# Tree levels in blocks of 64 keys by 32 queries, masked straight into place; the order around ring slots, the gate in the output weights and the last norm

## The chip, the cores and the metric

The kernel runs on one core of a Trainium2 chip. The metric is device time in microseconds (us) of one execution. Three runs of the kernel before took 2049.74 to 2051.89 us, median 2050.69 us.

## What is computed

One layer over 2048 tokens of width 1024, in float32. `proj = h @ w_in` makes queries, forget values and values for two paths of 8 heads each: a gated linear recurrence (HGRN2) and a retention with a fixed decay. Both are normed by head, gated, merged and sent through `w_out`; a last norm follows.

```
h    = rms_norm(x, norm_g) * (1 + scale) + shift      # shift, scale, gate from c
proj = h @ w_in
# HGRN2, by head:  S_t = diag(f_t) S_{t-1} + (1 - f_t) v_t^T ;  o_t = S_t^T q_t
#   inside a chunk:  A[t, s] = sum_d q[t,d] * decay[t,s,d] * k[s,d]   for s <= t
# retention, by head: the same with a fixed decay
m    = sigmoid(ga) * uA + sigmoid(gb) * uB
x    = x + gate * (m @ w_out)
out  = rms_norm(x, final_g)
```

## The kernel before

**Dense products.** All projections are 128x128 by 128x512 products on TensorE. A float32 number is split into a high and a low part (`hi` by ScalarE, `lo` by VectorE), and each product is three matmuls (`mm3`, lines 505 to 508). `x` is held in two super-blocks (`sb`) of 1024 tokens. For each of them and each of 4 pairs of heads (`p`), `do_pair` runs group `a` (forget values `gf` and queries `gq`), for even `p` group `b` (retention queries and keys of two pairs, `gr`), group `c` (values, `gv`) and two groups `d` (gates, `gg`). A group by tokens has 8 chunks of 128 tokens; one chunk is 24 matmuls into one of three PSUM banks (tag `pd`), and the last two chunks, 6 and 7, run side by side (`group_two`).

**The ring.** Weights come from HBM into two raw buffers and are split into a ring of 9 slots (`Ring.pump`). As chunk 7 uses up a slot, `release` calls `pump`, which splits a tile of the next group. In group `b` VectorE also reads the result out of PSUM by two products with cosines and sines (`rotate_products`, line 778); only then can the bank be used again. `tc.issue_after(i)` says that what is traced inside stands behind instruction `i` on that engine; what is not said so, a scheduler sorts.

**The tree.** Inside a chunk of 128 tokens the decay matrix of the recurrence is built in 7 levels, m = 1, 2, 4 ... 64 (`tree`, lines 584 to 697). At level m, the queries of each odd block of m tokens meet the keys of the even block before it; then VectorE multiplies `q` and `k` with the products of forget values in `f`, and the next level follows. The level's products go to the PSUM tile `lv` (one buffer). In code before, levels 1 to 8 multiply 32 keys with the 16 odd queries among the same 32 tokens: 64 matmuls for the 16 chunks of a pair, at 4 places of the array's columns (output rows 0, 32, 64, 96). Level 16 has 64 products of 16 keys by 16 queries at the same 4 places, level 32 has 32 products of 32 by 32 at 2 places, level 64 has 16 of 64 by 64 at 2 places. A mask `msk` keeps what belongs to a level: `copy_predicated` on VectorE writes it into `ad` (128 x 16 x 32), and at level 8 four copies on ScalarE put `ad` on the diagonal of `af` (128 x 16 x 128), the matrix that the recurrence's products read. Levels 16 to 64 go to `af` by copies on ScalarE.

**Between the dense matmuls.** `bg.tick` counts them, and at every ninth step a burst of small work is traced: a level of the tree, a step of the retention, a step of the recurrence. TensorE runs in this order, one behind the other.

**The end.** `out_half(t, nh)` multiplies the merged rows with one half of `w_out` (`ops`); VectorE multiplies the result with `gate`, adds it to `x`, ScalarE sums the squares, and at `nh == 1` follow the sum, a power -0.5 on GpSimd (`rstd_of`), two scalings on VectorE and two transfers. `load_wo(0)` is traced in the last group of gates and `load_wo(1)` behind the first two halves; the order of the halves is written out at line 1239.

Of the kernel before, what the change touches and what calls it, by code (L numbers as in the profile page):

```python
# [42 lines left out]
def tile_hybrid(ctx: ExitStack, tc: tile.TileContext, a: dict, out: bass.AP):  # L43
# [47 lines left out]
    def late_consts():  # L91
        m32 = upool.tile([P, 512], I32, name="m32", tag="sg", bufs=3)
        nc.sync.dma_start(out=m32[:, 0:66], in_=a["msk"])
        G.tensor_copy(
            out=msk, in_=m32[:, 0:64].rearrange("p (l t) -> p l t", l=4).unsqueeze(2).broadcast_to([P, 4, 16, 16])
        )
        G.tensor_copy(out=dmsk, in_=m32[:, 64:66].unsqueeze(1).broadcast_to([P, 16, 2]))
        for t, src in lates:
            nc.sync.dma_start(out=t, in_=src)
# [122 lines left out]
    msk = cpool.tile([P, 4, 16, 16], U8, name="msk", tag="msk")  # L222
    dmsk = cpool.tile([P, 16, 2], U8, name="dmsk", tag="dmsk")
# [6 lines left out]
    ad = cpool.tile([P, 16, 32], F32, name="ad", tag="ad")  # L230
    G.memset(ad, 0.0)
# [229 lines left out]
    class Ring:  # L461
        def __init__(self):
# [7 lines left out]
            self.lasts = []  # L470

# [27 lines left out]
        def release(self):  # L499
            self.nfree += 1  # L500
            self.pump()
# [82 lines left out]
    def tree(p, sb, f, k, q):  # L584
# [14 lines left out]
        for li in range(7):  # L599
# [11 lines left out]
            if m < 16:  # L611
                for c in range(NC):
                    for u in range(4):
                        t0 = c * P + u * 32
                        PE.matmul(
                            out=ps[32 * u : 32 * u + 32, c * 16 : (c + 1) * 16].rearrange("p (n m) -> p n m", m=m),
                            lhsT=k[:, t0 : t0 + 32],
                            rhs=q[:, t0 : t0 + 32].rearrange("p (n two m) -> p n two m", two=2, m=m)[:, :, 1, :],
# [3 lines left out]
            else:  # L622
                nr = 64 // m
                for n in range(NC * nr):
                    c, r0 = (n // nr, n % nr * 2 * m) if m < 64 else (n // 2, n % 2 * 64)
                    PE.matmul(
                        out=ps[r0 : r0 + m, c * m : (c + 1) * m], lhsT=km[:, n, 0, :], rhs=qm[:, n, 1, :],
# [14 lines left out]
            if m == 1:  # L642
                V.copy_predicated(
                    out=ad.rearrange("p c (w j) -> p c w j", w=2)[:, :, :, 0], mask=dmsk,
                    data=psd.rearrange("p (c w) -> p c w", w=2),
                )
            if m < 16:
                V.copy_predicated(
                    out=ad.rearrange("p c (n two m) -> p (c n) two m", two=2, m=m)[:, :, 1, :],
                    mask=msk[:, li].rearrange("p c (n m) -> p (c n) m", m=m),  # L650
                    data=ps[:, 0 : 16 * NC].rearrange("p (n m) -> p n m", m=m),
                )
# [6 lines left out]
            else:  # L659
                for r0 in range(0, P, 2 * m):  # L660
                    S.activation(
                        out=af[r0 : r0 + m, :, r0 + m : r0 + 2 * m],
                        in_=ps[r0 : r0 + m, 0 : NC * m].rearrange("p (c t) -> p c t", t=m), func=AF.Copy,
                    )
# [107 lines left out]
    def rotate_products(p, gc, ps):  # L772
# [4 lines left out]
        for dst, tab in ((qk, rot["cos"]), (tr, rot["sin"])):  # L777
            V.tensor_tensor(  # L778
# [4 lines left out]
            )  # L783
        return qk, tr
# [130 lines left out]
    def do_pair(sb, p, hook):  # L915
# [296 lines left out]
    def out_half(t, nh):  # L1212
# [13 lines left out]
        V.tensor_tensor(out=yt, in0=ps, in1=gate[nh], op=ALU.mult)  # L1226
        V.tensor_tensor(out=xt[nh], in0=xt[nh], in1=yt, op=ALU.add)
        S.activation(out=yt, in_=xt[nh], func=AF.Square, accum_out=ss[:, nh : nh + 1])
        if nh == 0:
            return  # L1230
# [117 lines left out]
```

## Time and profile before

| | |
|---|---|
| median of the runs shown | 2050.69 us |
| the profiled execution's own time | 2049.87 us |
| its span, first to last instruction | 2047.9 us |
| mean granted clock of TensorE | 0.998 |
| VectorE busy | 1076.9 us (53%) |
| matmuls of `q` and `k` on `lv` in one tree (a float32 product is two instructions in the trace) | 736 |

The profile is of one execution. Its span is 2.0 us below the time of that execution, which is in turn 0.8 us below the median. In its rows PE is TensorE's matmuls, PEld its weight loads, DVE is VectorE, ACT ScalarE, POOL GpSimd, SP the engine that issues the transfers. In a timeline, a row gives the start, the duration, engine, line, operation, output and inputs, and how many instructions it merges; the bracket holds the idle time ahead of it and what ended that.

### The profile page before, as it was taken

How to read it: one execution, taken by the hardware profiler on the slowest of the kernel's cores; microseconds unless marked ns; L12 is line 12 of the kernel's file. 1: busy time of each engine (PE TensorE's matmuls, PEld its weight loads, DVE VectorE, ACT ScalarE, POOL GpSimd, SP SyncE). 2: the span in 40 equal slices, each digit the busy share in tenths (PEclk: the TensorE clock that was granted, in tenths of full speed). 3: DMA queues.
4: the chain of work that ended last, by engine and by line, in shares of the span. 5: the costliest groups of instructions: out<-in, count | busy, mean ns of one | idle time of the engine just before them, and what ended most of it. 6: DMA issues, size and time to landing. Idle time of an engine off the chain costs nothing.

```text
span 2047.9 us, 38316 instructions
## 1 busy us (share of the span) xinstructions
PE 2029.0 (99%) x15480; PEld 1674.4 (82%) x15480; DVE 1076.9 (53%) x2409; ACT 590.6 (29%) x1429; POOL 145.2 (7%) x262
## 2 busy tenths in 40 slices
PE   8999999999999999999999999999999999999998
PEld 6887888888888888888888888888878888888886
DVE  7376634553465535557465535553555535566553
ACT  8412322322113222436123212322123222324221
POOL 1000100110001100120000100010000100010000
PEclk9999999999999999999999999999999999999999
DMA  8135321322344211434334211321333211347531
GB/s 321 42 80 130 81 55 53 90 58 52 74 120 102 64 48 54 99 106 143 77 97 99 65 50 55 88 61 50 87 96 100 67 48 54 89 114 220 185 129 62
DMA packets 312561, 187.66 MB, mean 92 GB/s; under 512 B 217664, under 2 KB 274496, under 8 KB 312384
## 3 DMA queue, kind: packets, MB, share of 16 engines
q1 hardware_dynamic: 312384, 185.22, 33.0%
q8 instruction: 121, 1.98, 0.4%
q14 instruction: 56, 0.46, 0.1%
HBM read 147.39 MB, written 37.75 MB: 90 GB/s over the span
## 4 chain that ended last, share of the span: by engine, by line
PE 91%; DMA 3%; issue 2%; DVE 2%; ACT 1%; SPq 1%; POOL 0%; DVEq 0%; POOLq 0%; ACTq 0%
PE gg L53 31%; PE gv L53 16%; PE gq L53 9%; PE gf L53 9%; PE ops L53 8%; PE gr L53 7%; PE poh L53 4%; PE lv L53 3%; PE por L53 3%; PE rt L53 2%; DMA wc<-in_w_c_dram 1%; DMA wd<-in_w_d_dram 1%; DMA wr<-in_w_o_dram 0%; DMA bad<-in_bada_t_dram 0%; DMA mr<-mT_dram 0%
## 5 line engine op out<-in xcount | busy, mean ns | idle before, releaser
L53 PE MATMUL gg<-whd,h 128*128 128x512 f32 x2048 | 656.2, 394 | 0.5 <-DVE tr L778 0.5
L53 PEld LDWEIGHTS gg<-whd,h 128*128 128x128 f32 x2048 | 385.1, 188 | 78.7 <-PE gg L53 0.9
L53 PE MATMUL gg<-wld,h 128*128 128x512 f32 x1024 | 399.2, 390 | 0.0
L53 PE MATMUL gv<-whc,h 128*128 128x512 f32 x1024 | 329.5, 397 | 2.6 <-DVE tr L778 1.9
L53 PEld LDWEIGHTS gv<-whc,h 128*128 128x128 f32 x1024 | 190.7, 188 | 43.1 <-ACT h L393 1.9
L53 PEld LDWEIGHTS gg<-wld,h 128*128 128x128 f32 x1024 | 192.8, 188 | 36.9 <-issue 0.2
L53 PE MATMUL gv<-wlc,h 128*128 128x512 f32 x512 | 193.4, 390 | 0.0
L53 PE MATMUL gr<-whb,h 128*128 128x512 f32 x512 | 160.2, 391 | 0.0
L53 PE MATMUL ops<-wo,mh 128*128 128x512 f32 x512 | 158.8, 391 | 0.2 <-DVE wo L1021 0.2
L53 PE MATMUL gq<-h,wha 128*128 128x512 f32 x512 | 157.8, 390 | 0.0
L53 PE MATMUL gf<-h,wha 128*128 128x512 f32 x512 | 157.7, 389 | 0.0
L883 ACT ACTIVATE sgg<-gg 128x512 f32<-128x512 f32 x128 | 75.4, 595 | 243.4 <-PE gg L53 242.9
L121 POOL TENSOR_TENSOR rrr<-ssr,mhalf 128x2 f32<-128x2 f32 x64 | 54.5, 852 | 1196.4 <-DVE ssr L120 1085.1
L494 DVE TENSOR_TENSOR wld<-wd,whd 128x512 fp32r<-128x512 f32 x128 | 86.3, 686 | 64.4 <-ACT whd L493 64.4
L53 PEld LDWEIGHTS ops<-wo,mh 128*128 128x128 f32 x512 | 96.2, 188 | 21.7 <-DVE wo L1021 1.0
L53 PEld LDWEIGHTS gf<-h,wha 128*128 128x128 f32 x512 | 96.2, 188 | 19.9
L53 PEld LDWEIGHTS gr<-whb,h 128*128 128x128 f32 x512 | 96.2, 188 | 19.9
L53 PEld LDWEIGHTS gq<-h,wha 128*128 128x128 f32 x512 | 96.1, 188 | 19.8
L53 PEld LDWEIGHTS gv<-wlc,h 128*128 128x128 f32 x512 | 96.4, 188 | 18.9
L493 ACT ACTIVATE whd<-wd 128x512 fp32r<-128x512 f32 x128 | 79.2, 630 | 98.8 <-DMA wd<-in_w_d_dram 57.6
L886 DVE TENSOR_TENSOR ga<-gg,sgg 128x256 f32<-128x256 f32 x128 | 52.6, 415 | 95.1 <-ACT sgg L883 93.2
L53 PE MATMUL gr<-wlb,h 128*128 128x512 f32 x256 | 99.8, 390 | 0.0
(161 smaller groups left out, 2758.1 us busy)
## 6 DMA issues: line engine op xcount, KB each, us to landing
wd<-in_w_d_dram SPq DMA_DIRECT2D x64, 512.0 KB, 3.7
wc<-in_w_c_dram SPq DMA_DIRECT2D x32, 512.0 KB, 3.8
wa<-in_w_a_dram SPq DMA_DIRECT2D x32, 512.0 KB, 3.7
wa<-in_w_ada_dram SPq DMA_DIRECT2D x16, 512.0 KB, 7.5
wb<-in_w_b_dram SPq DMA_DIRECT2D x32, 256.0 KB, 3.2
qkT<-tr SPq DMA_DIRECT2D x128, 64.0 KB, 1.9
rqk<-qkT SPq DMA_DIRECT2D x64, 128.0 KB, 2.3
dk<-f SPq DMA_DIRECT2D x16, 512.0 KB, 2.7
```

The lines of the kernel that those rows point to most:

```text
L53: made = nc.tensor.matmul(**kw)
L121: G.tensor_tensor(out=dst, in0=ss, in1=mhalf.broadcast_to([P, width]), op=ALU.pow)
L493: S.activation(out=hi, in_=w, func=AF.Copy)
L494: self.lasts.append(V.tensor_tensor(out=lo, in0=w, in1=hi, op=ALU.subtract).ins)
L883: S.activation(out=sg, in_=ps, func=AF.Sigmoid)
L886: V.tensor_tensor(out=ga, in0=ps[:, 0:256], in1=sg[:, 0:256], op=ALU.mult)
```

## The change

**Tree.** Levels 2 to 32 take 64 keys by 32 queries: 32 matmuls each, at 2 places of the array's columns (output rows 0 and 64). Level 1 and level 64 stay. The masks are laid out for that (`msk` 128 x 4 x 16 x 32, `dmsk` 128 x 16 x 4, set to zero first, filled from 32 partitions at a time), and `copy_predicated` writes levels 1 to 8 straight into `af`, in two halves of 64 partitions. `ad` and its four copies on ScalarE at level 8 go.

**Ring.** Two slots are kept free from chunk 5 of group `b` on; the cosine and sine products of chunks 6 and 7 stand behind the sixth split, and the last two splits behind these products.

**Output.** The weights are multiplied by `gate` on VectorE before they are split; the product with `gate` behind each half goes. At `nh == 0` the mean of the squares is scaled and `final_g` multiplied in. At `nh == 1` the squares of the last tile are summed on VectorE, GpSimd keeps only the power, and the two last scalings are one on ScalarE and one on VectorE. Four tiles, not three, do their first half ahead.

```diff
-            if m < 16:
+            if m == 1:
...
+            elif m < 64:
                 for c in range(NC):
-                    for u in range(4):
-                        t0 = c * P + u * 32
+                    for g in range(2):
+                        t0 = c * P + g * 64
                         PE.matmul(
-                            out=ps[32 * u : 32 * u + 32, c * 16 : (c + 1) * 16].rearrange("p (n m) -> p n m", m=m),
-                            lhsT=k[:, t0 : t0 + 32],
-                            rhs=q[:, t0 : t0 + 32].rearrange("p (n two m) -> p n two m", two=2, m=m)[:, :, 1, :],
+                            out=ps[64 * g : 64 * g + 64, c * 32 : (c + 1) * 32].rearrange("p (n m) -> p n m", m=m),
+                            lhsT=k[:, t0 : t0 + 64],
+                            rhs=q[:, t0 : t0 + 64].rearrange("p (n two m) -> p n two m", two=2, m=m)[:, :, 1, :],
...
             if m < 16:
-                V.copy_predicated(
-                    out=ad.rearrange("p c (n two m) -> p (c n) two m", two=2, m=m)[:, :, 1, :],
-                    mask=msk[:, li].rearrange("p c (n m) -> p (c n) m", m=m),
-                    data=ps[:, 0 : 16 * NC].rearrange("p (n m) -> p n m", m=m),
-                )
+                for r in halves:
+                    a = af[r, :, r]
...
+                        V.copy_predicated(
+                            out=a.rearrange("p c (n two m) -> p c n two m", two=2, m=m)[:, :, :, 1, :],
+                            mask=msk[r, li].rearrange("p c (n m) -> p c n m", m=m),
+                            data=ps[r, 0 : 32 * NC].rearrange("p (c n m) -> p c n m", c=NC, m=m),
+                        )
...
-            if m == 8:
-                for r0 in range(0, P, 32):
-                    S.activation(out=af[r0 : r0 + 32, :, r0 : r0 + 32], in_=ad[r0 : r0 + 32], func=AF.Copy)
...
-                    with tc.issue_after(ring.lasts[-3]):
+                    with tc.issue_after(ring.lasts[-1 if ring.kept else -3]):
                         made.append((p, sb * CH + c, *rotate_products(p, sb * CH + c, ps)))
+                    if c == CH - 3:
+                        ring.kept = 2
+                    if c == CH - 1:
+                        ring.kept = 0
+                        with tc.issue_after(rot["last"]):
+                            ring.pump()
...
+                V.tensor_tensor(out=w[:, i, :], in0=w[:, i, :], in1=gate[nh], op=ALU.mult)
                 S.activation(out=hi, in_=w[:, i, :], func=AF.Copy)
...
-        V.tensor_tensor(out=yt, in0=ps, in1=gate[nh], op=ALU.mult)
-        V.tensor_tensor(out=xt[nh], in0=xt[nh], in1=yt, op=ALU.add)
-        S.activation(out=yt, in_=xt[nh], func=AF.Square, accum_out=ss[:, nh : nh + 1])
+        V.tensor_tensor(out=xt[nh], in0=xt[nh], in1=ps, op=ALU.add)
+        if t < L // P - 1 or nh == 0:
+            S.activation(out=yt, in_=xt[nh], func=AF.Square, accum_out=ss[:, nh : nh + 1])
+        else:
+            V.tensor_tensor_reduce(
+                out=yt, in0=xt[nh], in1=xt[nh], scale=1.0, scalar=0.0, op0=ALU.mult, op1=ALU.add, accum_out=ss[:, 1:2]
+            )
...
+        V.scalar_tensor_tensor(out=r[:, 0:1], in0=ss[:, 1:2], scalar=1.0 / D, in1=ss[:, 0:1], op0=ALU.mult, op1=ALU.add)
+        G.tensor_tensor(out=r[:, 0:1], in0=r[:, 0:1], in1=mhalf, op=ALU.pow)
+        S.activation(out=xt[0], in_=xt[0], func=AF.Copy, scale=r[:, 0:1])
+        V.scalar_tensor_tensor(out=xt[1], in0=xt[1], scalar=r[:, 0:1], in1=fg[1], op0=ALU.mult, op1=ALU.mult)
...
-    order = [(t, nh) for nh in range(2) for t in range(3)] + [(t, nh) for t in range(3, L // P) for nh in range(2)]
+    order = [(t, nh) for nh in range(2) for t in range(4)] + [(t, nh) for t in range(4, L // P) for nh in range(2)]
```

Where the instructions stand shows best in the order in which each engine takes them. First TensorE, around level 2 of the first tree (`lv0_0_2`), in the middle of the third chunk of the first group `b` (`gr0_2`). Before:

```order
L53 MATMUL gr0_2_1250<-wlb21_1060,h0_5_440 128x512
L53 MATMUL gr0_2_1250<-whb21_1059,h0_5_440 128x512
L53 MATMUL lv0_0_2_1274<-q0_0_819,k0_0_818 32x16 x64
L53 MATMUL gr0_2_1250<-whb22_1068,h0_6_497 128x512
L53 MATMUL gr0_2_1250<-wlb22_1069,h0_6_497 128x512
```

And in the change:

```order
L53 MATMUL gr0_2_1258<-wlb21_1066,h0_5_440 128x512
L53 MATMUL gr0_2_1258<-whb21_1065,h0_5_440 128x512
L53 MATMUL lv0_0_2_1282<-q0_0_825,k0_0_824 64x32 x32
L53 MATMUL gr0_2_1258<-whb22_1074,h0_6_497 128x512
L53 MATMUL gr0_2_1258<-wlb22_1075,h0_6_497 128x512
```

The level stands at the same place between the same dense matmuls; 64 products of 32 keys by 16 queries are now 32 products of 64 by 32.

Next VectorE, at the same level: `L636`, `L637` and `L640` bring `q` and `k` to the next level, `L641` the products of forget values. Before:

```order
L636 TENSOR_TENSOR q0_0_819<-q0_0_819,f0_0_817 128x512x2
L637 TENSOR_TENSOR k0_0_818<-k0_0_818,f0_0_817 128x512x2
L648 COPY_PREDICATED ad_107<-msk_100,lv0_0_2_1274 128x128x2
L640 TENSOR_TENSOR k0_0_818<-k0_0_818,f0_0_817 128x128
L778 TENSOR_TENSOR qk0_2_1350<-gr0_2_1250,cos0_813 128x512
L641 TENSOR_TENSOR f0_0_817<-f0_0_817 128x4x128
```

In the change, where these lines are 649, 650, 653 and 654:

```order
L649 TENSOR_TENSOR q0_0_825<-q0_0_825,f0_0_823 128x512x2
L650 TENSOR_TENSOR k0_0_824<-k0_0_824,f0_0_823 128x512x2
L671 COPY_PREDICATED af_107<-msk_100,lv0_0_2_1282 64x16x16x2
L653 TENSOR_TENSOR k0_0_824<-k0_0_824,f0_0_823 128x128
L671 COPY_PREDICATED af_107<-msk_100,lv0_0_2_1282 64x16x16x2
L654 TENSOR_TENSOR f0_0_823<-f0_0_823 128x4x128
```

One masked copy of 256 elements in a partition has become two of 512, one of them ahead of the last update of `k`.

Last VectorE at the end of the first group `b`, where `wld24` to `wld31` are the low parts of the next group's 8 weight tiles, `wld32` the first of the one behind it, and the products read chunks 6 and 7 (`gr0_6`, `gr0_7`). Before:

```order
L494 TENSOR_TENSOR wld30_1824<-wd3_3_1755,whd30_1823 128x512
L494 TENSOR_TENSOR wld31_1834<-wd3_3_1755,whd31_1833 128x512
L778 TENSOR_TENSOR qk0_6_1849<-gr0_6_1632,cos0_813 128x512
L494 TENSOR_TENSOR wld32_1846<-wd4_0_1777,whd32_1845 128x512
L778 TENSOR_TENSOR tr0_6_1850<-gr0_6_1632,sin0_815 128x512
L778 TENSOR_TENSOR qk0_7_1853<-gr0_7_1633,cos0_813 128x512
L778 TENSOR_TENSOR tr0_7_1854<-gr0_7_1633,sin0_815 128x512
```

In the change:

```order
L499 TENSOR_TENSOR wld30_1715<-wd3_3_1646,whd30_1714 128x512
L799 TENSOR_TENSOR qk0_6_1718<-gr0_6_1543,cos0_819 128x512
L799 TENSOR_TENSOR tr0_6_1719<-gr0_6_1543,sin0_821 128x512
L799 TENSOR_TENSOR qk0_7_1722<-gr0_7_1544,cos0_819 128x512
L799 TENSOR_TENSOR tr0_7_1723<-gr0_7_1544,sin0_821 128x512
L499 TENSOR_TENSOR wld31_1727<-wd3_3_1646,whd31_1726 128x512
L499 TENSOR_TENSOR wld32_1733<-wd4_0_1706,whd32_1732 128x512
```

The four products have moved ahead of two splits; the split of `wld31`, the last tile that the next group needs, has moved behind them.

More of the change, by code (lines that the diff above doesn't have):

```diff
@@ L220, in tile_hybrid @@
     gate = {}
-    msk = cpool.tile([P, 4, 16, 16], U8, name="msk", tag="msk")
-    dmsk = cpool.tile([P, 16, 2], U8, name="dmsk", tag="dmsk")
+    msk = cpool.tile([P, 4, 16, 32], U8, name="msk", tag="msk")
+    dmsk = cpool.tile([P, 16, 4], U8, name="dmsk", tag="dmsk")
+    G.memset(msk, 0)
+    G.memset(dmsk, 0)
     epsx = const_("epsx", [P, H], a["epsx"])
@@ L470, in __init__ @@
             self.lasts = []
+            self.kept = 0
         def load(self, upto):
@@ L500, in release @@
             self.nfree += 1
-            self.pump()
+            self.pump(RING - self.kept)
     ring = Ring()
@@ L622, in tree @@
             else:
-                nr = 64 // m
-                for n in range(NC * nr):
-                    c, r0 = (n // nr, n % nr * 2 * m) if m < 64 else (n // 2, n % 2 * 64)
+                for n in range(NC):
+                    g = n % 2
                     PE.matmul(
-                        out=ps[r0 : r0 + m, c * m : (c + 1) * m], lhsT=km[:, n, 0, :], rhs=qm[:, n, 1, :],
+                        out=ps[64 * g : 64 * g + 64, n // 2 * 64 : n // 2 * 64 + 64], lhsT=km[:, n, 0, :], rhs=qm[:, n, 1, :],
                         start=True, stop=True,
@@ L783, in rotate_products @@
             )
+        rot["last"] = made.ins
         return qk, tr
```

46 lines of the change are left out of this document (30 added, 16 removed).

## The prediction

> **What bounds the kernel.** I read the page's busy times first, then the chain of work that ended last, then the waits of TensorE.
>
> ```profile
> span 2047.9 us, 38316 instructions
> ...
> PE 2029.0 (99%) x15480; PEld 1674.4 (82%) x15480; DVE 1076.9 (53%) x2409; ACT 590.6 (29%) x1429; POOL 145.2 (7%) x262
> ...
> PE 91%; DMA 3%; issue 2%; DVE 2%; ACT 1%; SPq 1%; POOL 0%; DVEq 0%; POOLq 0%; ACTq 0%
> ...
> 72.32 5.44 PE gf L53 x24
> ...
> PE gv L53 <- DVE tr L778: 1.9, 2, 1.3
> ...
> PE gg L53 <- DVE tr L778: 0.5, 1, 0.5
> ...
> PE ops L53 <- DVE wo L1021: 0.2, 1, 0.2
> ```
>
> TensorE works for 99% of the span and is 91% of the chain. Past the start it waits for other engines three times for `tr` and once for `wo`, 2.6 us in all. A dense chunk is 24 matmuls in 5.44 us, one every 0.227 us. So the time is what stands in TensorE's queue: a microsecond added to a tree level, which lies between two dense matmuls, is a microsecond of the kernel, while VectorE and ScalarE can take work until TensorE waits for it. I go by what each edit does to that queue.
>
> **1. The tree levels.** They make up the large term. Busy times of single levels of the first tree, levels 2, 16, 32 and 64 in this order; each window runs from the level's first matmul to the next dense one (its columns: window, length, PE busy, PEld busy):
>
> ```profile
> 132.25:133.45 1.20, 1.19 (x128) 1.17 (x128) 0.00 (x0) 0.00 (x0) 1.00 0.03 7
> 154.93:156.09 1.16, 1.15 (x128) 1.12 (x128) 0.00 (x0) 0.00 (x0) 1.00 0.72 124
> 162.43:163.57 1.14, 1.13 (x64) 1.09 (x64) 0.00 (x0) 0.00 (x0) 1.00 0.93 294
> 177.24:178.33 1.09, 1.08 (x32) 1.01 (x32) 0.00 (x0) 0.00 (x0) 1.00 0.65 112
> ```
>
> A float32 product is two instructions, each with its own weight load. Count them by place in the array: level 2 has 128 on 4 places, level 32 has 64 on 2, so both go through 32 rounds of 32-column loads. They take nearly the same, 1.20 and 1.14 us, though level 32 streams 32 queries for each load and level 2 only 16. Level 64 has 32 on 2 places: 16 rounds of 64-column loads in 1.09 us. Apart from level 16, time goes with rounds times loaded columns; level 16 has 128 instructions with 16 columns each, and 0.009 us apiece seems to be the least they take. For the changed level's 64 instructions that floor is 0.58 us. The heads of such bursts show why; narrow windows of the timeline cut them after one round and after the next:
>
> ```profile
> 132.26 0.13 PEld L53 LDWEIGHTS lv<-q,k 128*32 128x32 f32 x4 [0.35 <-issue]
> ...
> 132.26 0.16 PEld L53 LDWEIGHTS lv<-q,k 128*32 128x32 f32 x8 [0.35 <-issue]
> ...
> 185.09 0.14 PEld L53 LDWEIGHTS rt<-v,rkz 128*64 128x64 f32 x2
> ...
> 185.09 0.20 PEld L53 LDWEIGHTS rt<-v,rkz 128*64 128x64 f32 x4
> ...
> 185.10 0.44 PE L53 MATMUL rt<-v,rkz 128*64 128x128 f32 x4
> ...
> 177.25 0.14 PEld L53 LDWEIGHTS lv<-q,k 128*64 128x64 f32 x2
> ...
> 177.25 0.20 PEld L53 LDWEIGHTS lv<-q,k 128*64 128x64 f32 x4
> ...
> 177.25 0.31 PEld L53 LDWEIGHTS lv<-q,k 128*64 128x64 f32 x7
> ```
>
> Four loads of 32 columns end 0.03 us after the four before them, one for each place. Two loads of 64 columns end 0.06 us after the two before, with 64 columns streamed (`lv`) as with 128 (`rkz`). The seventh load belongs to the fourth round and ends 0.31 - 0.14 = 0.17 us after the first, so a round of 64 columns is 0.057 us. A place of the array is kept by its load, for 0.03 us at 32 columns and 0.057 at 64; the streaming is hidden behind it.
>
> The changed levels 2 to 32 have 32 products, 64 instructions, on 2 places: 32 rounds of 64-column loads, twice level 64. The trace has no such level with 32 queries, so it is bounded. Below: if the streamed columns set the time (32 x 32 = 1024, as 16 x 64 in level 64), a level takes 1.09 us, and a tree gains 3 x 0.11 + 0.07 + 0.05 = 0.45 us, 3.6 us in 8 trees. Above: 16 rounds more than level 64, at 0.057 us, 1.09 + 0.91 = 2.00 us. I take this end, to which the `rkz` row is nearest: its loads follow one another at 64 columns' pace with a quite different stream. Then a tree loses 3 x 0.80 + 0.84 + 0.86 = 4.1 us, and 8 trees **+32.8 us**. Fewer instructions do not help, because four levels had four places at work and would have two.
>
> [...]
>
> **2. The masked copies.** VectorE has two copies of 512 elements for one of 256 at each of four levels, and two small ones for one.
>
> ```profile
> 135.86 0.74 DVE L648 COPY_PREDICATED ad<-msk,lv 128x256 f32<-128x256 uint8 x1
> 136.38 0.44 DVE L640 TENSOR_TENSOR k<-k,f 128x128 f32<-128x128 f32 x1
> ...
> 143.43 0.43 DVE L648 COPY_PREDICATED ad<-msk,lv 128x256 f32<-128x256 uint8 x1
> 143.75 0.40 DVE L640 TENSOR_TENSOR k<-k,f 128x128 f32<-128x128 f32 x1
> ...
> 121.00:156.00 35.00, 35.00 (x773) 28.53 (x771) 31.93 (x55) 3.15 (x5) 0.00 (x0) 1.00 0.36 80
> ```
>
> From start to next start a copy costs 0.52 us at level 2 (and, I take it, at level 1) and 0.32 at level 4 (and 8). Four times the elements: 3 x 0.52 x 2 + 3 x 0.32 x 2 = 5.0 us a tree, 5.3 with the small ones. The tightest place is the first tree, where VectorE is busy for 31.93 of 35 us (third number with an x) beside the first group `b`. Its 3.1 free microseconds and the 4 x 0.8 by which term 1 lengthens it are 6.3, so 5.3 fit: **0**. If copies in this form take twice that, 10.6 - 6.3 = 4.3 us of waiting, the upper end. ScalarE, at 29%, has nothing to gain from the four copies that go. GpSimd's eight small casts for two are early, ahead of the first tree, and cost 0.
>
> **3. The ring.** What the products' old place cost, and what comes after:
>
> ```profile
> 1496.27 0.39 PE L53 MATMUL gv<-whc,h 128*128 128x512 f32 x1
> 1497.92 0.47 PE L53 MATMUL gv<-whc,h 128*128 128x512 f32 x1 [1.26 <-DVE tr L778]
> ...
> 1493.61 1.29 DVE L494 TENSOR_TENSOR wlc<-wc,whc 128x512 fp32r<-128x512 f32 x2 [2.41 <-ACT whc L493]
> ...
> 1497.09 0.68 DVE L778 TENSOR_TENSOR tr<-gr,sin 128x512 f32<-128x512 f32 x1
> 1497.69 0.68 DVE L778 TENSOR_TENSOR qk<-gr,cos 128x512 f32<-128x512 f32 x1
> ...
> 1491.05 0.39 PE L53 MATMUL gv<-whc,h 128*128 128x512 f32 x1
> ...
> 576.55 1.29 DVE L494 TENSOR_TENSOR wlc<-wc,whc 128x512 fp32r<-128x512 f32 x2 [2.46 <-ACT whc L493]
> ...
> 574.93 0.39 PE L53 MATMUL gv<-whc,h 128*128 128x512 f32 x1
> ...
> 169.69 1.29 DVE L494 TENSOR_TENSOR wld<-wd,whd 128x512 fp32r<-128x512 f32 x2 [2.20 <-ACT whd L493]
> ...
> 167.79 0.39 PE L53 MATMUL gg<-whd,h 128*128 128x512 f32 x1
> ```
>
> The bracket says 1.26 us, the starts 1.65 where 0.23 is usual: 1.42 lost. With 0.15 more than the bracket each, the three waits cost 2.4 + 0.45 = 2.85 us. In the change the products come right behind the sixth split, the bank is free in time, and these waits go. But the eighth weight tile's low part, second of the two splits in each DVE row, now comes behind four products. It is ready one split (0.60), four products (4 x 0.60) and its own 0.69 after that row's start, 3.69 us; TensorE asks for it with its 23rd matmul, 22 x 0.227 = 4.99 us after the group's first. So the new wait is 1493.61 + 3.69 - 1491.05 - 4.99 = 1.26 us in the last group, and likewise 0.32 and 0.60 in the two others, 2.2 us in all. The fourth group `b`, which did not wait before, comes out about even. Net **-0.7 us**; -2.9 if nothing waits, +0.5 if the fourth waits too.
>
> **4. The last norm.** From the last dense matmul on, nothing hides anything:
>
> ```profile
> 2040.02 0.69 DVE L1226 TENSOR_TENSOR y<-ops,gate 128x512 f32<-128x512 f32 x1 [4.02 <-PE ops L53]
> 2040.75 0.69 DVE L1227 TENSOR_TENSOR xo<-xo,y 128x512 f32<-128x512 f32 x1
> ...
> 2042.28 0.16 DVE L1232 TENSOR_TENSOR or<-oss 128x1 f32<-128x1 f32 x1 [0.85 <-ACT y L1228]
> ...
> 2042.81 0.54 POOL L121 TENSOR_TENSOR or<-or,mhalf 128x1 f32<-128x1 f32 x1
> 2043.38 1.41 DVE L1235 SCALAR_TENSOR_TENSOR xo<-xo,or,fgs 128x512 f32<-128x512 f32 x2 [0.94 <-POOL or L121]
> 2044.16 0.99 SPq L1236 DMA_DIRECT2D out_dram<-xo  x2
> ```
>
> Before, the second scaling ends at 2044.79. After: the add ends its turn at 2040.75, the squares on VectorE (as long as an add, 0.69, and a short read) at 2041.5, the small sum at 2041.7, the power (0.54) at 2042.35, and both scalings, side by side, at 2043.1. The second transfer is issued half of 0.99 us behind the first, at 2043.6: **-1.2 us**. Bounds -1.7 (both at once) and -0.6 (squares twice as long).
>
> **5. The gate and the order of halves.** Sixteen products of 0.69 us go to VectorE ahead of the splits of `w_out`, 32 of the same length leave it. The tile's wait for its transfer moves from ScalarE to VectorE, and behind it queue the gates' products, which free TensorE's banks; three banks of 5.44 us each cover that. The second half's weights come later by their 8 products, 5.5 us, and are asked for 5.44 us later, since a fourth tile goes ahead. The 0.2 us for `wo` go: **-0.2 us**, up to +2 if the cover in the last gates fails.
>
> **Sum.** 32.8 - 0.7 - 1.2 - 0.2 = +30.7 us. The profiled execution took 2049.87 us, its span of 2047.9 and 2.0 around it, and lies 0.8 below the median of the runs shown; with the sum it is **2081 us**, 1.5% slower.
>
> **Rivals.** *Streamed columns set a level's time.* Then term 1 is -3.6, and all else -2.1: 2044 us, the other side. It decides if a place can take its next 64-column load in the time of 32 streamed columns, under 0.03 us. For it: levels 32 and 64 alone could be read so. Against it: level 2 streams half of what level 32 does in the same time, and the `rkz` loads. 8%. *Instructions set it.* Level 2 has 128 in 1.20 us, level 16 as many in 1.16; at that price halving them saves 0.6 us at four levels, 19 us in 8 trees: 2029 us. Against it, level 32 has half of level 2's instructions and takes 0.06 us less. 2%. [...] *VectorE becomes the bound as well*: the copies at twice their price in the first tree and the gate's cover gone, 4.3 + 2 us on the forecast, 2087 us. 8%. The forecast keeps 82%.
>
> **How the numbers follow.** The forecast's low end has rounds of 0.055 us, as the two decimals of the rows allow (a level of 1.94 us, term 1 at 30.4), no new wait in the ring (-2.9) and both last transfers at once (-1.7): 2049.87 + 25.6, some 2075; I set 2074. Its high end is the third rival's 2087, which the range takes in. Outside are the first two rivals, 10%, and about 7% beyond either end, so 2074 to 2087 should hold the time 8 times in 10. A measurement of this kernel can tell about 0.2% (4 us) from no change. The first rival's 2044 is 6 us below, and its own terms 3 and 5 can cost it 2 or more, so I give 5 of its 8% to faster and 3 to the same; the second rival's 2% are faster, and another 2% stands for a forecast that falls so low that it is no change. Faster 0.07, same 0.05, slower 0.88.
>
> **What would show it.** Loads of 64 columns on `lv` should number 2816 for 256, and a window over a changed level read about 2.0 us; 1.1 would mean the first rival, 0.6 the second. The waits for `tr` should be gone, with waits of `gv` and `gg` for the low part of a weight tile in their place. Waits of `lv` for VectorE would show term 2 wrong, waits of `gg` or `ops` in the last 180 us term 5.

## Result and profile after

The change makes the kernel slower: 2077.32 us median (2076.32 to 2077.75), against 2050.64 us for the kernel before on the same chip. The ratio is 1.0126, its 95% interval 1.0114 to 1.0138. The forecast was 2081 us, the range 2074 to 2087.

The page of the profile after, its span, its busy times and the packets of the instruction queue, which the experiments need (the numbers are the packets, megabytes and the share of 16 engines' span):

```profile
span 2075.9 us, 34256 instructions
...
PE 2057.5 (99%) x13432; PEld 1706.3 (82%) x13432; DVE 1119.8 (54%) x2451; ACT 582.2 (28%) x1411; POOL 142.6 (7%) x253
...
q8 instruction: 105, 1.72, 0.4%
```

TensorE has 2048 matmuls fewer, and its busy time is 28.5 us longer; the profiled execution took 2077.75 us, 27.9 more than that of before. Windows over single levels, as in the prediction: levels 2, 16, 32 and 64 of the first tree, then 2, 4, 32 and 64 of the second (window, length, PE, PEld, DVE):

```profile
133.45:135.44 1.99, 1.99 (x65) 1.95 (x65) 1.93 (x4) 0.00 (x0) 0.00 (x0) 1.00 0.05 8
158.44:160.43 1.99, 1.99 (x65) 1.95 (x64) 1.96 (x5) 0.00 (x0) 0.00 (x0) 1.00 0.04 8
166.82:168.81 1.99, 1.99 (x66) 1.95 (x65) 1.19 (x3) 0.00 (x0) 0.00 (x0) 1.00 0.78 169
181.70:182.78 1.08, 1.08 (x34) 1.01 (x32) 0.57 (x2) 0.00 (x0) 0.00 (x0) 1.00 0.79 126
343.36:345.35 1.99, 1.99 (x66) 1.95 (x64) 0.62 (x2) 0.00 (x0) 0.00 (x0) 1.00 0.14 39
353.54:355.48 1.94, 1.94 (x68) 1.90 (x64) 0.68 (x2) 0.00 (x0) 0.00 (x0) 1.00 0.37 106
382.47:384.40 1.93, 1.93 (x68) 1.90 (x64) 0.68 (x2) 0.00 (x0) 0.00 (x0) 1.00 0.68 244
392.11:393.14 1.03, 1.03 (x36) 0.96 (x32) 1.03 (x2) 0.33 (x1) 0.00 (x0) 1.00 0.71 290
```

A changed level takes 1.99 us in the first tree and 1.94 in the others, mostly; before it was 1.14 to 1.20. Level 64 is as it was. Summed over all 56 levels, each from its first product to the next product of another tile, that is 66.70 us before and 97.55 after, 30.85 more. Everything else together gives 2.9 us of the span back.

What TensorE waits for, in the view of its waits after (total, times, longest):

```profile
PE scp L53 <- DVE dgs L171: 5.4, 1, 5.4
...
PE gv L53 <- DVE wlc L499: 0.9, 1, 0.9
PE lv L53 <- issue: 0.9, 1, 0.9
...
PE lv L53 <- DVE af L665: 0.6, 1, 0.6
```

No row for `tr` is left, and none for `wo`. New are a wait for the low part of a weight tile (`wlc`) and one of a level for a copy into `af`.

### The profile page after: what moved, and what is told of

It is laid out like the page before. It is cut to its first block, busy times and chain, and to the rows that moved or that the text cites. A ratio compares the mean times of both kernels' runs of the same rounds, so it can differ in the third digit from the quotient of the medians.

```text
span 2075.9 us, 34256 instructions
## 1 busy us (share of the span) xinstructions
PE 2057.5 (99%) x13432; PEld 1706.3 (82%) x13432; DVE 1119.8 (54%) x2451; ACT 582.2 (28%) x1411; POOL 142.6 (7%) x253
## 4 chain that ended last, share of the span: by engine, by line
PE 96%; DVE 1%; ACT 1%; SPq 0%; DMA 0%; issue 0%; POOL 0%; POOLq 0%; DVEq 0%; ACTq 0%
PE gg L53 34%; PE gv L53 16%; PE ops L53 8%; PE gf L53 8%; PE gq L53 8%; PE gr L53 7%; PE lv L53 4%; PE poh L53 4%; PE por L53 3%; PE rt L53 2%; DVE wa L192 0%; PE xps L57 0%; DMA wc<-in_w_c_dram 0%; DMA wb<-in_w_b_dram 0%; PE scp L53 0%
## 5 line engine op out<-in xcount | busy, mean ns | idle before, releaser
L124 POOL TENSOR_TENSOR rrr<-ssr,mhalf 128x2 f32<-128x2 f32 x64 | 49.5, 773 | 1227.7 <-DVE ssr L123 1122.3
L908 DVE TENSOR_TENSOR ga<-gg,sgg 128x256 f32<-128x256 f32 x128 | 52.7, 415 | 94.5 <-ACT sgg L905 92.6
L53 PE MATMUL lv<-q,k 128*64 128x32 f32 (+2 forms) x3840 | 99.9, 212 | 1.5 <-issue 0.9
```

Source lines behind the costliest of these rows:

```text
L53: made = nc.tensor.matmul(**kw)
L124: G.tensor_tensor(out=dst, in0=ss, in1=mhalf.broadcast_to([P, width]), op=ALU.pow)
L908: V.tensor_tensor(out=ga, in0=ps[:, 0:256], in1=sg[:, 0:256], op=ALU.mult)
```

## Experiments

Times are medians, beside the kernel before on the same chip. "tree" is the part of the change in the levels, masks and copies; "the rest" is the ring, the output and the last norm.

| run | median us | kernel before | ratio, 95% interval |
|---|---|---|---|
| no_tree: the change, tree as before | 2048.22 | 2050.63 | 0.9985, 0.9976 to 0.9995 |
| tree_only: before, tree of the change | 2080.35 | 2050.63 | 1.0136, 1.0121 to 1.0151 |
| lv32_keys: before, level 32 loads 64 keys | 2056.38 | 2050.63 | 1.0025, 1.0015 to 1.0034 |
| four_places: the change, 32 keys on four places | 2068.64 | 2050.63 | 1.0079, 1.0062 to 1.0095 |
| four_shift: that, 32 matmuls more at the start | 2070.42 | 2050.18 | 1.0097, 1.0083 to 1.0111 |
| spread: no_tree, levels 32 and 64 on four places | 2042.71 | 2050.18 | 0.9966, 0.9952 to 0.9979 |
| spread_shift: that, 64 matmuls more at the start | 2045.41 | 2050.56 | 0.9973, 0.9964 to 0.9981 |
| spread32: no_tree, level 32 alone on four places | 2047.98 | 2051.24 | 0.9984, 0.9975 to 0.9993 |
| spread32_shift: that, 64 matmuls more | 2047.20 | 2050.56 | 0.9987, 0.9978 to 0.9996 |

Three probes of level 64 were run once each, so they have no interval; each leaves out a part of the level's products. Only their windows are read, below.

### The change in two parts

```diff
# no_tree, against the change (tree_only takes the other half)
-            elif m < 64:
-                for c in range(NC):
-                    for g in range(2):
...
+            if m < 16:
+                for c in range(NC):
+                    for u in range(4):
...
-                for r in halves:
-                    a = af[r, :, r]
+                V.copy_predicated(
+                    out=ad.rearrange("p c (n two m) -> p (c n) two m", two=2, m=m)[:, :, 1, :],
```

> The change without its tree: levels, masks, copies into ad and the four copies on ScalarE as before; ring, gate in the weights, last norm and order as in the change. Theory (loads of 64 columns on two places cost the time): the 30.4 us of the levels go, and the rest shows what the other edits give, about -4 us on the kernel before, 2046.5 us. Rival (the rest of the change costs part of it, by the ring or the gate): not below 2050 us. The first group's products at the start: if the memset of af beside VectorE slowed them in the change, their time is still that of before here, since ad and af are set as before.

> The kernel before with the tree of the change alone: 64 keys by 32 queries, masks and copies into af; ring, gate, last norm and order as before. Theory: +30.4 us for the levels, +0.6 for a wait at level 2 of the first tree, +0.5 at the start, about 2082 us. If the gains of the other edits need the tree (or are eaten by it), the sum of this run's and the other part's differences misses the change's +27 us by more than 2 us.

The tree alone costs 29.7 us, and the rest alone gains 2.4; the sum, 27.3, is near the 26.7 of the whole, so the parts do not need each other. `no_tree` missed its 2046.5 by 1.7 us. In its profiled execution the level windows add up to 68.34 us instead of 66.70, by stalls that a later section explains; but that execution took 2050.78 us, 2.6 over the median, so why the median missed is not shown. As to the start, `dgs` is waited for as long as before (4.1 us) in `no_tree` and 5.4 with the memset of `af` beside it. The first group `a` begins at 72.59 us there, against 72.71 after and 72.16 before; without that memset or a shift other executions begin at 72.14 to 72.58, and `four_places`, with it, at 72.18, so no cost of the memset is shown.

### Loaded columns alone doubled

```diff
+                    kn = kk[:, n * 64 : n * 64 + 64] if m == 32 else km[:, n, 0, :]
                     PE.matmul(
-                        out=ps[r0 : r0 + m, c * m : (c + 1) * m], lhsT=km[:, n, 0, :], rhs=qm[:, n, 1, :],
+                        out=ps[r0 : r0 + (64 if m == 32 else m), c * m : (c + 1) * m], lhsT=kn, rhs=qm[:, n, 1, :],
```

> The kernel before with one size changed: at level 32 each of the 32 products loads 64 keys instead of 32. The count of products, their 32 queries, the two places and everything on the other engines stay; the 32 extra output rows are not read. Theory (the loaded columns on a place set a level's time): level 32 goes from 1.14 to 1.94 us, 8 x 0.80 = 6.4 us more, 2057 us. Rival, streamed columns set it: no change, level 32 at 1.14. Rival, instructions set it: no change as well, since there are 64 as before. Rival, copies or VectorE: no change.

It cost 5.75 us. Level 32 in the second tree, before and in this run, in the view of windows:

```profile
374.92:376.06 1.14, 1.14 (x66) 1.09 (x64) 0.68 (x2) 0.00 (x0) 0.00 (x0) 1.00 0.79 323
```

```profile
376.18:378.11 1.93, 1.93 (x68) 1.90 (x64) 0.68 (x2) 0.00 (x0) 0.00 (x0) 1.00 0.62 240
```

The same 64 matmuls, the same 32 queries, the same two places: only the load is twice as wide, and the level has the time of the change's levels. That rules out the first two rivals of the prediction, the streamed columns and the count of instructions, for this shape.

### The change on four places

```diff
-                    for g in range(2):
-                        t0 = c * P + g * 64
+                    for u in range(4):
+                        t0 = c * P + u // 2 * 64
...
-                            out=ps[64 * g : 64 * g + 64, c * 32 : (c + 1) * 32].rearrange("p (n m) -> p n m", m=m),
-                            lhsT=k[:, t0 : t0 + 64],
+                            out=ps[32 * u : 32 * u + 32, c * 32 : (c + 1) * 32].rearrange("p (n m) -> p n m", m=m),
+                            lhsT=k[:, c * P + u * 32 : c * P + u * 32 + 32],
```

> The change with its products of levels 2 to 32 split in two: 32 keys by 32 queries, 64 products on four places instead of 32 on two. Masks, copies, 32 queries for each product, ring and output as in the change. Theory (loaded columns on a place): 32 rounds of 32-column loads again, 1.14 to 1.20 us a level for 1.94, 40 levels x 0.76 = 30 us less than the change, 2047 us. Rival, the 32 streamed queries for 16 made levels longer: it stays at 2077. Rival, the copies into af: it stays at 2077. Rival, instructions: twice as many, so longer than the change.

The time missed the expectation by 22 us, and yet the levels did what was expected. Windows over level 2 and level 32 of the second tree:

```profile
344.22:345.44 1.22, 1.21 (x128) 1.18 (x128) 0.62 (x2) 0.00 (x0) 0.00 (x0) 1.00 0.09 28
...
382.60:383.82 1.22, 1.22 (x130) 1.19 (x128) 0.68 (x2) 0.00 (x0) 0.00 (x0) 1.00 0.82 332
```

Level 2 streams 32 queries for the 16 of before and takes 1.22 us for 1.20. What was gained here was lost inside other levels. TensorE's timeline at level 8 of the first tree, then windows over the stall and over the dense products behind it (the last three numbers of a window are the granted clock, the DMA share and GB/s), and the total in the view of waits:

```profile
149.01 1.20 PE L53 MATMUL lv<-q,k 128*32 128x32 f32 x119
152.70 0.27 PE L53 MATMUL lv<-q,k 128*32 128x32 f32 x9 [2.48 <-issue]
152.90 0.50 PE L53 MATMUL gr<-whb,h 128*128 128x512 f32 x1
```

```profile
150.04:152.70 2.66, 0.18 (x22) 0.08 (x8) 2.62 (x7) 0.00 (x0) 0.00 (x0) 1.00 0.07 20
153.90:157.30 3.40, 3.40 (x9) 2.63 (x8) 3.37 (x5) 0.00 (x0) 0.00 (x0) 0.50 0.53 103
```

```profile
PE lv L53 <- issue: 11.3, 8, 2.5
```

After 119 of 128 products TensorE stops for 2.5 us with nothing to wait for ("issue"). Then the granted clock falls to 0.50, and for 3.4 us a dense product takes 0.43 us instead of 0.23. Eight such stalls stand in its levels, and two of them, of 2.7 and 2.1 us, are followed by the half clock. Level windows add up to 80.57 us: 17.0 less than in the change, where 40 levels x 0.72 = 28.8 were due. From the first group `a` to the first product of `ops`, all but the levels took 7.8 us more than in the change. The two half clocks are about 3.2 us of that (an estimate: 3.4 us each, at 0.43 us for 0.23 a product), and longer waits, among them a second one for VectorE in the first tree (0.6 us, at level 4), about 1.4; some 3 us stay open.

### What TensorE runs out of

Here a weight load and its matmul count as two instructions (the prediction and the expectations mostly count the pair as one), and the queue named "instruction" brings one packet for 128 pairs in each kernel: 105 packets for 13432 matmuls after, and here:

```profile
q8 instruction: 125, 2.05, 0.4%
```

That is 15992 matmuls in 125 packets, 16 KB each. Counting matmuls from 0 at the program's start, these are the last ones before each stall in a level (with the time from that start to the next, and the number's remainder by 128):

```
four_places   1114 2.68us 90 | 2768 1.69 80 | 6205 0.37 61 | 6715 1.31 59 | 8365 2.72 45 | 8874 1.03 42 | 10659 1.01 35 | 12312 2.09 24
four_shift     987 2.68us 91 | 2768 0.98 80 | 5313 0.60 65 | 6715 1.02 59 | 12185 3.41 25 | 12695 0.72 23 | 14480 0.96 16
no_tree       4293 0.52us 69 | 8109 0.70 45 | 13330 1.28 18
spread32      8109 0.43us 45 | 13330 2.62 18
before       11926 0.42us 22 | 13327 0.59 15
after        11538 1.09us 18
```

The remainder falls through the run, by 0.7 to 0.8 in each 128 of `four_places` and `four_shift`, as if a block of 256 held one or two instructions that are not in the list of matmuls. Different kernels stall at the same count: `four_places` and `four_shift` at 2768 and 6715, though the shift puts another product of the burst there, `no_tree` and `spread32` at 8109 and 13330.

The packets in the trace say it more directly. In each of these 23 stalls one packet of the queue "instruction" ended 1.0 to 1.6 us before TensorE went on. In some of the longest that packet only began after the stall had: by 0.1 us at 1114 of `four_places`, by 1.0 at 12185 of `four_shift`. So TensorE went on a short time, much the same each time, behind the arrival of its next instructions.

```diff
-        warm(8)
+        warm(8, 16)
...
+        for i in range(extra):
+            PE.matmul(out=ps[0:32, 0:16], lhsT=ident[:, 0:32], rhs=ident[:, 0:16], start=True, stop=True)
```

> The kernel with 64 products on four places, with 16 small products (32 instructions) more at its very start, 1 us or less beside other work. That kernel had levels of 1.22 us, as expected, but 8 of its levels held a stall of 0.4 to 2.7 us without a releaser, 12 us in all, each at a product whose number among TensorE's matmuls is near the end of a block of 128 (256 instructions, 16 KB, the size of a packet of the instruction queue). Theory, TensorE runs out of instructions there: the stalls leave the levels in which they were (level 8 of the first tree, level 4 of the second and so on) and come, if at all, 32 instructions earlier in the stream of work, so in levels 4, 8, 8, 2, 16, 2 and 16 of trees 1, 5, 6, 7, 7, 8 and 8; levels without one stay at 1.22; the time moves by up to 12 us to either side. Rival, an operand or a PSUM tile comes late (copies into af, VectorE): the stalls stay in the same levels, and the time stays at 2068.6.

The stalls stayed at the blocks' ends and so came 32 matmuls earlier in the work: level 4 of the first tree now has the 2.68 us, and six of the eight levels that had one lost it. Of the seven levels named, four got one; three others (level 4 of tree 2, level 32 of tree 3, level 8 of tree 4) were not named, so where a block's end must lie in a burst to hurt is not settled. A cause in the operands is ruled out. The time stayed within 2 us because about as much stall came as went: the level windows add up to 78.61 us, 2.0 less, and two stalls of the same kind, of 1.55 and 1.65 us, stand outside the levels.

### More places: a faster version

```diff
# level 32; n counts its 32 products
-                    c, r0 = (n // nr, n % nr * 2 * m) if m < 64 else (n // 2, n % 2 * 64)
+                    c, u = n // 2, n % 2 * 2 + n // 2 % 2
                     PE.matmul(
-                        out=ps[r0 : r0 + m, c * m : (c + 1) * m], lhsT=km[:, n, 0, :], rhs=qm[:, n, 1, :],
+                        out=ps[32 * u : 32 * u + 32, c // 2 * 32 : c // 2 * 32 + 32], lhsT=km[:, n, 0, :], rhs=qm[:, n, 1, :],
# level 64, in spread alone: 32 of 32 x 64 for 16 of 64 x 64
+                        u, lh, rh, o = c % 2 * 2 + e, km[:, c, 0, 32 * e : 32 * e + 32], qm[:, c, 1, :], c // 2 * 64
```

> The change without its tree, and levels 32 and 64 of the tree before spread over all four places: level 32 has the same 64 instructions of 32 keys by 32 queries, a chunk with an even number at rows 0 and 64, one with an odd number at rows 32 and 96; level 64 has 64 instructions of 32 keys by 64 queries for 32 of 64 by 64. Theory (a place is kept by its loaded columns, and places work side by side): 16 rounds of 32-column loads at 0.03 us, which is below 64 instructions at 0.009, so some 0.6 us for each of both levels, for 1.14 and 1.03; 8 x (0.54 + 0.45) = 8 us less than without the spread (2048.2), 2040 us, plus or minus 2 for instruction supply. Rival, streamed columns: level 32 as before or 0.57, level 64 stays at 1.03, since a place still streams 1024 columns. Rival, instructions: level 32 stays at 1.14.

Levels 32 and 64 of the second tree in `spread`:

```profile
374.79:375.48 0.69, 0.69 (x66) 0.65 (x64) 0.57 (x2) 0.00 (x0) 0.00 (x0) 1.00 0.77 309
383.31:384.34 1.03, 1.03 (x66) 0.94 (x64) 0.72 (x2) 0.80 (x2) 0.00 (x0) 1.00 0.90 350
```

Level 32 gained 0.45 us of the expected 0.54, and the time, 2042.71 us, missed the 2040 by 2.7. Level 64 gained nothing, although each place now loads 32 columns for 64. So the theory as first stated, loads alone, does not hold there. Three probes cut level 64 on the kernel before.

```diff
+                    if m == 64:
+                        kn, qn, w = kn[:, 0:32], qn[:, 0:64], 64
...
# l64_q32: 0:64 and 0:32, w = 32; l64_both: 0:32 and 0:32, w = 32
```

> The kernel before, with level 64 cut in one size: 32 of its 64 keys by all 64 queries, 32 instructions on two places as before; the other 32 keys of each chunk are left out. The level takes 1.03 us before. Theory as first stated (a place is kept by its loaded columns, streaming is hidden): 16 rounds at 0.03, 0.55 us. New theory (a place is kept by the longer of loaded and streamed columns): 64 are still streamed, so 1.03. Either way the run's time moves by 4 us at most.

> The kernel before, with level 64 cut in the other size: all 64 keys by 32 of its 64 queries; the other queries are left out. First theory (loaded columns alone): 1.03 us, as before. New theory (the longer of the two): 64 are still loaded, so 1.03. Streamed columns alone: 0.55.

> The kernel before, with level 64 cut in both sizes, 32 keys by 32 queries; the rest is left out. First theory: 0.55 us. New theory: 16 rounds of 0.03 and some 0.1 at the end, 0.55 to 0.65. If a round of two places has a floor of its own that is not in the columns, the level stays near 1.03.

Level 64 of the second tree before, then in the three runs, in this order:

```profile
383.77:384.80 1.03, 1.03 (x36) 0.97 (x32) 0.92 (x2) 0.59 (x2) 0.00 (x0) 1.00 0.83 338
```

```profile
385.27:386.29 1.02, 1.02 (x34) 0.93 (x32) 1.02 (x2) 0.48 (x1) 0.00 (x0) 1.00 0.50 205
```

```profile
384.26:385.27 1.01, 1.01 (x36) 0.97 (x32) 0.83 (x2) 0.67 (x2) 0.00 (x0) 1.00 0.83 337
```

```profile
384.33:384.96 0.63, 0.63 (x34) 0.59 (x32) 0.63 (x2) 0.38 (x1) 0.00 (x0) 1.00 0.99 403
```

Half the keys or half the queries: no gain. Half of both: 0.40 us less. All shapes together, windows from above and from the prediction:

| level, run | columns loaded | streamed | matmuls for each place | us |
|---|---|---|---|---|
| 64, l64_both | 32 | 32 | 16 | 0.63 |
| 32, spread | 32 | 32 | 16 | 0.69 |
| 32, before | 32 | 32 | 32 | 1.14 |
| 2, four_places | 32 | 32 | 32 | 1.22 |
| 64, l64_keys32 and spread | 32 | 64 | 16 | 1.02, 1.03 |
| 64, l64_q32 | 64 | 32 | 16 | 1.01 |
| 64, before | 64 | 64 | 16 | 1.03 |
| 32, lv32_keys | 64 | 32 | 32 | 1.93 |
| 2 to 32, after | 64 | 32 | 32 | 1.94 |

In these rows a place is kept for the longer of the two: (1.14 - 0.63) / 16 = 0.032 us where it is 32, (1.94 - 1.01) / 16 = 0.058 us where it is 64. Below 32 columns the rule does not go on: level 16 before, with 16 loaded, 16 streamed and 32 matmuls for each place, takes 1.16 us in the prediction's row, as much as levels with 32.

> The version meant to be kept: the change without its tree, and level 32 alone spread over four places; level 64 as before, since its spread left it at 1.03 us. Level 32 takes 0.69 us for 1.14, 8 x 0.45 = 3.6 us less than the change without its tree: 2044.6 us from that run's 2048.2, and 2042 to 2043 if it has as few stalls of instruction supply as the run with both levels spread.

> The version with level 32 alone on four places, and 32 small products (64 instructions) more at the very start, some 2 us that stand beside waits for transfers. It had 2047.98 us, with a stall of 2.6 us in level 1 of the last tree at a block's end, and 1.9 us of waits of the retention's products for VectorE. Theory (instruction supply): the block's end in that level moves 64 instructions forward, to the middle of the burst, and the stall goes; level 1 of the last tree reads 1.28 us for 3.92, and the whole lies up to 3 us lower, unless other levels (those whose block's end lay 35 to 63 instructions in: some ten) get stalls of their own. Rival (the stall belongs to that place of the program, by its operands): it stays, and the time with it.

> The fastest version so far (levels 32 and 64 on four places, 2042.71 us against 2050.18), with the same 64 small instructions more at the start. That version had next to no stall in its levels (0.3 us in all). If its lead over the version with level 32 alone is only the lucky place of the blocks' ends, this run loses it and comes to 2045 to 2048; if it is the spread of level 64 itself, it stays at 2043 to 2044, though that level's window did not change.

Level 32 took 0.69 us in all four runs. `spread32` should have won 3.6 us over `no_tree` and won 0.2 by its medians. Its profiled execution has a 2.6 us stall in level 1 of the last tree, but took 1.5 us more than the median, so how many executions have that stall is not known. With the shift the stall went, as expected; level 1 of the last tree, first without and then with it, in the timeline:

```profile
1705.18 1.21 PE L53 MATMUL lv<-q,k 128*32 128x16 f32 x123
1708.84 0.25 PE L53 MATMUL lv<-q,k 128*32 128x16 f32 x5 [2.44 <-issue]
```

```profile
1705.75 1.27 PE L53 MATMUL lv<-q,k 128*32 128x16 f32 x128
```

but the median fell by 0.8 us only, and beside the kernel before, on each chip, nothing was won (3.3 us under it, then 3.4). `spread` is the fastest kernel of the study, with and without the shift: 0.27 to 0.34% under the kernel before, 1.5 to 1.7% under the change. Its lead of 1.8 us or more over level 32 alone is not explained by level 64's window. The shifted run lost 2.3 us of what it had won, and its 2045.41 us lies where the expectation put a lucky place of the blocks' ends. But its level windows add up to 62.41 us, against 62.39 without the shift, so no stall in a level did it. In the profiled executions the first group `a` begins 0.6 us later, and the waits for low parts of weight tiles are 3.0 us instead of 1.1. The two shifted profiles differ by 1.1 us, 0.6 in the levels' stalls and 0.6 at the start. A gain from the spread of level 64 is thus not shown.

## Why the prediction was right

**Term 1, the levels: +32.8 predicted, 30.85 measured.** The round of 0.057 us was right: nearly everywhere a changed level is 0.91 us longer than level 64 in its own tree, 16 rounds of 0.057. Mis-sized was the base. It was read from the first tree, where level 64 takes 1.08 us and a changed level 1.99, and was used for all eight; in the others level 64 and 32 of the 35 changed levels are 0.05 lower, and 32 x 0.05 = 1.6 us is most of the 2 us missing. The 30.85 also hold 0.1 of stalls, 0.5 more in the last level 1 and 0.4 less elsewhere. The low end of the forecast, 1.94 us a level and 30.4 us in all, came nearer by luck: the later trees' 1.94 us is a base of 1.03 us and 16 rounds of 0.057, not a shorter round. The 30.4 us that the expectations count for the levels is the same number from the windows after, 40 levels x 0.76 (1.94 for 1.14 to 1.20).

One argument for the term was misread, though the end it was to choose was right. The `rkz` loads were taken as a round of 64 loaded and 128 streamed columns in 0.06 us. But the loads ran ahead of their products there: all four had ended at 185.29 us. TensorE's rows of the kernel before, in the same window as these loads, cut at 185.20:

```profile
185.10 0.33 PE L53 MATMUL rt<-v,rkz 128*64 128x128 f32 x2
```

Only two products have begun by then, and with all four the prediction's row reads 0.44: 0.11 us for a round of 128 streamed columns, as far as the modelled ends of matmuls can be trusted. "The streaming is hidden behind it" holds for the change, which loads 64 and streams 32, and not as a rule: by the probes it is the longer one that counts.

**Term 2, the copies: 0 predicted, 0.6 measured.** `lv` waits once for `af`, at level 2 of the first tree, the tightest place that the prediction named, well under the 4.3 us of its upper end. `tree_only` has VectorE busy for 52.7 us more than before, 6.6 a tree where 5.3 was worked out; the 6.3 us of cover fell a little short.

**Term 3, the ring: -0.7 predicted, not separated from the scatter.** The first product of `ops` in the kernel before, in `tree_only` and after, and then the last one in the same three:

```profile
1864.18 0.80 PE L53 MATMUL ops<-wo,mh 128*128 128x512 f32 x1
...
2039.59 0.39 PE L53 MATMUL ops<-wo,ml 128*128 128x512 f32 x1
```

```profile
1895.17 0.79 PE L53 MATMUL ops<-wo,mh 128*128 128x512 f32 x1
...
2069.47 0.39 PE L53 MATMUL ops<-wo,ml 128*128 128x512 f32 x1
```

```profile
1894.30 0.79 PE L53 MATMUL ops<-wo,mh 128*128 128x512 f32 x1
...
2068.60 0.39 PE L53 MATMUL ops<-wo,ml 128*128 128x512 f32 x1
```

With the same tree, the rest of the change brings the output 0.87 us forward. One pair of executions does not make that the ring's work: with the tree of before, the stretch from the first group `a` to the first product of `ops`, less the level windows, is 1725.3 us before and 1726.5 in `no_tree`, the other way. The waits can be counted in all profiles. Those for `tr` and for low parts, from the first group `a` on, add up to 1.5 to 3.2 us in the six with the order of before and to 0.8 to 3.0 in the eight with the new one. The means differ by 0.7, as forecast, but the ranges overlap. In the change itself the new waits for a low part are 0.9 us in one place and 0.15 in another, for 2.2 forecast in three.

**Term 4, the last norm: -1.2 predicted, -1.0 measured.** From the last product to the end of the span it is 2075.91 - 2068.60 = 7.31 us after, and 8.35 before and 8.39 in `tree_only`. The rows after, from VectorE's add on:

```profile
2069.02 0.69 DVE L1256 TENSOR_TENSOR xo<-xo,ops 128x512 f32<-128x512 f32 x1 [3.15 <-PE ops L53]
2069.74 0.69 DVE L1260 CUSTOM_DVE_ANT_0 y<-xo 128x512 f32<-128x512 f32 x1
2070.36 0.08 DVE L1260 DVE_READ_ACCUMULATOR2_ANT oss<- 128x1 f32 x1
...
2070.78 0.54 POOL L1270 TENSOR_TENSOR or<-or,mhalf 128x1 f32<-128x1 f32 x1 [10.32 <-DVE or L1269]
2071.36 0.72 ACT L1271 ACTIVATE xo<-xo,or 128x512 f32<-128x512 f32 x1 [6.27 <-POOL or L1270]
2071.36 0.75 DVE L1272 SCALAR_TENSOR_TENSOR xo<-xo,or,fgs 128x512 f32<-128x512 f32 x1 [0.72 <-POOL or L1270]
```

The squares take 0.69 us on VectorE, as an add does, and the two scalings run side by side, as worked out.

**Term 5, the gate: -0.2 predicted, -1.1 measured.** Between the first and the last product of `ops` lie 175.41 us before, 174.30 after, and 174.30 also in `tree_only`, where the output is as before. The forecast counted only the 0.2 us of one idle row. Before, five products at that place start 0.33 to 0.73 us behind the one ahead, where 0.23 is usual; together they hold 1.0 of the 1.1. What they wait for comes from the last transfer of `w_out`: ScalarE takes it up 1883.16 - 1864.18 = 18.98 us after the first product before, and 1912.43 - 1895.17 = 17.26 in `tree_only`:

```profile
1883.16 1.15 ACT L1020 ACTIVATE wo<-wr 128x512 fp32r<-128x512 f32 x2 [4.63 <-DMA wr<-in_w_o_dram]
```

```profile
1912.43 1.15 ACT L1040 ACTIVATE wo<-wr 128x512 fp32r<-128x512 f32 x2 [4.44 <-DMA wr<-in_w_o_dram]
```

In `tree_only` that transfer came earlier by itself, and 1.1 us went without the edit. In the five other profiles with the output of before the stretch takes 175.2 to 175.6 us, in all eight with the new output 174.30. So with the tree of before the new output does bring about 1.1 us; with the tree of the change one execution did without it.

So the forecast of +30.7 became +28.0 in the span. The levels gave +30.85 for 32.8, the rest up to the output -1.3 for -0.7, the output -1.1 for -0.2, the last norm -1.0 for -1.2, and the start +0.55, which the forecast left out (without the change the starts lie up to 0.45 apart). The levels, which decide the sign and nearly all of the size, came out as worked out; the small terms missed on both sides.

## What to carry to other kernels

Before small products are merged, count for each place of the array the matmuls times the longer of loaded and streamed columns (measured here for 32 and 64): halving the matmuls was worth nothing here, where it also halved the places that work (1.94 us a level for 1.14 to 1.20). Spreading the same products over more places is the better direction: level 32 of this kernel went from 1.14 to 0.69 us. A burst of 128 tiny matmuls is also a burst of 256 instructions, and their supply stalled in eight levels of `four_places`, 11.3 us in all; look at the packets of the queue "instruction" where an "issue" wait stands inside such a burst.

## What was not expected of the hardware

In these runs TensorE outran its instructions: 256 of them in 1.22 us (level 2 of `four_places`), against packets of 16 KB that each bring 256 (125 packets for 15992 matmuls and as many loads), with stalls of 0.4 to 3.4 us at blocks' ends, each over 1.0 to 1.6 us after such a packet had come. In `four_places` that was 11.3 us.

A stall of 2.1 us or more could be followed by 3.4 us at a granted clock of 0.50 (153.90 to 157.30 us in `four_places`; 6.8 us behind the stall of 3.4 us in `four_shift`); 3.4 us of it cost another 1.6 us or so, by the same estimate as above. Some stalls of 2.6 and 2.7 us had none behind them. Within a run all changes of the granted clock lie whole multiples of one step apart, to 0.004 us; the step is 3.41333 us (594 steps in 2027.517 us before, 597 in 2037.756 after). In `four_places` and `four_shift` each of the four falls came at the end of such a step in which a stall had taken 2.07 us or more (2.18, 2.09, 2.68 and 2.07). The stalls without a fall, of 2.73 us in `four_places` and 2.62 in `spread32`, lay across two steps, with 1.71 and 1.01, and 1.37 and 1.26 us in them. A threshold is not shown by that: near the start a fall to 0.50 came behind a step in which TensorE was busy for 2.14 of 3.41 us before (it lasts from 13.56 to 16.98) and for 1.82 after (29.78 to 33.20), so with 1.27 and 1.59 us idle.
